# Five drains of GpSimd's DMA queue: four among the expert blocks, one behind the tail's gather

## The chip, the core and the metric

The kernel runs on one core of a Trainium2 chip. A core has a matrix engine (PE, with its weight loads as PEld), a vector engine (DVE), a scalar engine (ACT), GpSimd (POOL), a queue that mostly issues transfers (SP), and 16 DMA engines that all of these feed. The metric is the device time of one execution in microseconds (us), lower is better. A change is told from no change here when the median moves by more than about 0.5%, which is 5.9 us.

## The reference

The program computes one residual block of a streaming encoder for 512 tokens of width 1024 in float32: a layer norm, a token mixer (a gated MLP branch and a gated delta-rule branch, merged through gates), a second layer norm, a mixture of experts, and a last layer norm. Only the mixture of experts and the norm behind it matter here:

```
pg  = softmax(x @ w_rg + b_rg)            # one of 4 groups per token
le  = (x @ w_re + b_re) of that group     # 8 experts, the best two are taken
gate = p_group * softmax(top two logits)
y   = silu(x @ w1[e]) * (x @ w3[e]) @ w2[e]   for the two experts e of each token
out = sum over the two of gate * y
h   = LayerNorm(alpha * h + out)
```

There are 32 experts with 1024 x 512, 1024 x 512 and 512 x 1024 weights in float32, so 6 MB of weights each.

## The kernel before

The first half of the program (to about 676 us) is the token mixer, the norm behind it and the router, which sorts the experts by load and makes the lists of token indices. Then `Experts.run` goes through 32 expert blocks. For each it loads six 1 MB pieces of weights on SP's queue, gathers the block's token rows from `h1_dram` (`fetch`, L1605, an indirect DMA that POOL issues into one of the tiles called `mh`), turns them around on PE (`turn_x`, L1631), multiplies (`up`, L1659), applies the gate (`gate`, L1668), multiplies again (`down`, L1690), copies the result into the tile `once` (L1717 on DVE, L1722 on ACT) and scatters its rows to `y_rows` in DRAM (`store_y`, `scatter`, L1697, indirect DMAs that POOL issues). The order on each engine in this part is the order in which the code is written.

POOL's work here is nearly all DMA issues. In iteration b of the loop it meets, in this order: `fetch(b+3, 0)`, the gather of the first 64 rows of the block three ahead; for some blocks `fetch(b+2, 1)`, a further gather of up to 96 rows, which stands in a conditional and is skipped where the block has at most 64 tokens (L1602; the branch that skips it holds an instruction INC_SWDGE_SEM, which makes up the semaphore counts of the gather that was left out); and the scatters of block b-1. Blocks of even number from 4 to 26 are "short": they scatter 32 rows with one DMA (its index list is `itail`), the others up to block 27 use three DMAs (`itail` and twice `islot`), and the last four blocks none, since their results stay on the chip.

From block 25 on, `Tail` joins in. At (29, 1), that is at the end of iteration 29, it starts to add the experts' rows up: ACT's queue reads `y_rows` back in four pieces, and POOL gathers one more set of rows of it into `mh` (L1764, the helper's line is L1794). Behind that gather on POOL stand only small power operations for the last layer norm (L1838) and, at the very end, the scatter of the last 128 rows to `out` (L1788).

After the tail, each engine reads a flag and branches (L2028, L2029) past a part for token counts that the fixed plan doesn't hold; that part isn't entered with these inputs. On POOL the branch not entered also has an INC_SWDGE_SEM. Then comes the end of the program (L2120), where every engine has DRAIN instructions and a barrier.

Of the kernel before, what the change touches and what calls it, by code (L numbers as in the profile page):

```python
# [41 lines left out]
FEW = range(4, 28, 2)  # L42
TURNS = ((3, 4, 21, 1, 7), (5, 4, 20, -1, 6), (4, 2, 14, -1, 4), (12, 2, 3, 1, 8))
OOB = 1e4


C_BU, C_BQ, C_BK, C_BV, C_BZ, C_BGA, C_BGB = (8 * i for i in range(7))
# [1112 lines left out]
class Router:  # L1160
# [234 lines left out]
    def rows(self, W, idx2, n, slot, tail):  # L1395
# [10 lines left out]
        for q in range(2):  # L1406
            v.tensor_scalar(y[64 * q:64 * q + 64], x[0:64], 2.0, q + OOB, op0=OP.mult, op1=OP.add)
        v.scalar_tensor_tensor(out=slot, in0=m, scalar=-OOB, in1=y, op0=OP.mult, op1=OP.add)
        t = W.tile([32, 3, w], F32, name="rt%d" % w)
# [43 lines left out]
class Experts:  # L1453
# [30 lines left out]
    def clear(self):  # L1484

        for t in [self.u[:, p] for p in range(NP)] + [self.y0[:, 0:256]] + self.y:
            n = t.shape[1] // 128
            self.nc.scalar.activation(out=t.rearrange("p (a n) -> p a n", a=n), in_=bc(self.cst["ident"], n, 1),
                                      func=AF.Copy, scale=0.0)

    def run(self, blocks, more=None, clear=None, tail=None):

        nc, kk, nb = self.nc, self.kk, len(blocks)
        steps = []
        for b in range(nb + 1):
            steps += [(b, c) for c in range(4)] if b < nb else []
            steps += [(b - 1, 4), (b - 1, 5)] if b else []
        if clear:  # L1500
            steps[0:14] = steps[1:14] + steps[0:1]
        conds, self.raw, todo = {}, {}, iter(steps)

        def load(n, always=False):
            for _, (b, c) in zip(range(n), todo):
                blk = blocks[b]
                if blk[5] and not always and b not in conds:
                    m = nc.values_load(blk[4][0], engines=(ET.SP,), min_val=0, max_val=NB,
                                       skip_runtime_bounds_check_because="counts of tokens")
                    conds[b] = m > 0  # L1510
                self.raw[b, c] = kk.load_big(blk[1]()[c], conds.get(b), self.once if clear and b + c == 0 else None)
                self.last, self.prior = kk.loaded, self.last

        more = more or iter(())
        self.blocks, self.s = blocks, [{} for _ in blocks]
        self.short = lambda b: bool(tail) and (b >= E - NL or b in FEW)
        if clear:
            load(15, True)
            load(1, True)
            kk.behind(self.last, [kk.normed])  # L1520
            load(2, True)
        else:
            load(len(kk.raws), True)
        if clear:
            for x in self.x:
                nc.gpsimd.memset(x[:, :, NA:96], 0.0)
            self.s[0]["r"], self.s[1]["r"] = [None], [None]
        for b in range(2 if clear else 0, min(3, nb)):
            self.fetch(b, 0)
        if clear:  # L1530
            clear()
        next(more, None)
        self.fetch(0, 1)

        self.turn_x(0, (lambda: self.up(0, None)) if clear else None)
        if not clear:
            next(more, None)
        if nb > 1:
            self.fetch(1, 1)
        for b in range(nb + 1):  # L1540
            if b + 3 < nb:
                self.fetch(b + 3, 0)
            if tail and b >= RT:
                tail(b, 0)
            if b < nb:
                self.parts(b, self.up)
                if tail and b in (RT, RT + 3):
                    n = kk.nraw % len(kk.raws)
                    kk.raws = kk.raws[n:] + kk.raws[:n]
                    self.spare, kk.raws, kk.nraw = kk.raws[0:2], kk.raws[2:], 0  # L1550
                    load(2)
                else:
                    load(3 if clear and b == 0 else 4)
                if clear and b == 0:
                    self.turn_x(1)
                elif clear and b == 1:
                    self.turn(0)
                self.gate(b)
            if clear and b == 0:
                next(more, None)  # L1560
            elif b + 1 < nb:
                self.turn_x(b + 1)
            if b + 2 < nb and not self.short(b + 2):
                self.fetch(b + 2, 1)
            next(more, None)
            if b:
                self.parts(b - 1, self.down)
                load(2)
            next(more, None)
            if b < nb and not (clear and b == 0):  # L1570
                self.turn(b)
            if b and not (tail and b == nb):
                self.store_y(b - 1, tail)
            next(more, None)
            if tail and b >= RT:
                tail(b, 1)
# [153 lines left out]
class Tail:  # L1730
# [8 lines left out]
    def __call__(self, b, at):  # L1739
        nc, kk, ex, r = self.nc, self.kk, self.ex, self.r  # L1740
        v, g, act, m = nc.vector, nc.gpsimd, nc.scalar, 128 - 32
        if (b, at) == (RT, 1):
            (self.g, self.b), (self.F, ex.Y) = ([x[:, i * D:(i + 1) * D] for i in range(2)] for x in ex.spare[0:2])
            act.dma_start(out=ex.Y[0:4], in_=kk.a["rows"][R_L1G:R_L2B + 1, :])
            v.memset(self.F, 0.0)
            self.gather(r.lgate, r.gd_dram, r.lidx2, 2 * T)
            self.gather(self.F, self.h1_dram, r.lidx, T)
        elif (b, at) == (RT + 1, 1):
            self.spread(0, ALPHA)
        elif b == RT + 2:  # L1750
            self.affine(self.f[2 * at:2 * at + 2])
        elif (b, at) == (RT + 3, 0):
            self.affine([self.F])
        elif (b, at) == (RT + 3, 1):
            self.spread(2, 1.0)
        elif (b, at) == (RT + 4, 0):
            self.y = ex.spare
            kk.behind(self.load(0), ex.stores)
            self.load(1)
        elif (b, at) == (RT + 4, 1):  # L1760
            self.add(0, 1)
            self.load(2)
            self.load(3)
            self.gather(self.O, self.y_dram, r.lother, 2 * T)  # L1764
        elif (b, at) == (RT + 5, 0):
            self.apply((0, 1), self.stats(0, 1))
        elif (b, at) == (RT + 5, 1):
            self.add(2, 3)
            v.scalar_tensor_tensor(out=self.F, in0=self.O, scalar=r.lgate[:, 1:2], in1=self.F, op0=OP.mult, op1=OP.add)
        elif (b, at) == (RT + 6, 0):  # L1770
            self.m = self.stats(2, 3)
        elif (b, at) == (RT + 6, 1):
            self.apply((2, 3), self.m)
            for t in range(NT):
                kk.stores.append(nc.sync.dma_start(out=kk.a["out"][t * 128:(t + 1) * 128, :], in_=self.f[t]))
                if t == 0:
                    kk.behind(kk.stores[0], [ex.prior])
            v.scalar_tensor_tensor(out=self.F[0:m], in0=ex.Y[0:m], scalar=r.lgate[0:m, 0:1], in1=self.F[0:m],
                                   op0=OP.mult, op1=OP.add)
        elif (b, at) == (E, 2):  # L1780
            F = self.F
            for q in range(4):
                f = F[m:128, q * 256:(q + 1) * 256]
                v.scalar_tensor_tensor(out=f, in0=ex.end[q * 32:(q + 1) * 32, 0:256], scalar=r.lgate[m:128, 0:1], in1=f,  # L1784
                                       op0=OP.mult, op1=OP.add)
            (rs, mean), = self.stats(F)
            self.norm(F, rs, mean)
            x = g.indirect_dma_start(out=kk.a["out"], out_offset=bass.IndirectOffsetOnAxis(ap=r.lidx, axis=0), in_=F,  # L1788
                                     in_offset=None, bounds_check=T - 1, oob_is_err=False)
            kk.behind(x, kk.stores)  # L1790
            kk.stores.append(x)
# [332 lines left out]
```

## Time and profile before

| | us |
|---|---|
| three timed runs | 1184.94, 1183.8, 1179.16 |
| their median | 1183.8 |
| the profiled execution's own time | 1181.13 |
| its span, first to last instruction | 1179.3 |
| PE busy in the span | 1048.8 (89%) |
| POOL busy in the span | 210.4 (18%) |
| DMA engines' share of the time, 870 to 1031 us | 1.02, at 402 GB/s |

The span is what the rows of the trace cover, and 1.8 us of the execution's time lie outside it. A row of a group gives a line of the code, the engine, the operation, the tiles written and read, the count, and the durations. Engine names with a q (POOLq, SPq) are the instructions of that engine's queue which aren't counted as busy: semaphore waits, branches, drains, DMA issues of SP and ACT. Rows of one line's instructions give minimum, median and maximum duration in ns and then the first and last start in us. Rows in order of time begin with start and duration in us; in brackets stands the time for which the engine sat idle before it, and what ended it. A DMA that POOL issues shows on POOL with the time of its issue alone; when its data has landed is seen from those who wait for it.

### The profile page before, as it was taken

The numbers are of one execution on the slowest core, as the hardware profiler recorded it, in microseconds if no ns is written. First come the engines' busy times: TensorE is split into PE (matmuls) and PEld (weight loads), VectorE is DVE, ScalarE is ACT, GpSimd is POOL, SyncE is SP. The second block draws the span as 40 slices with busy tenths as digits, with TensorE's granted clock in tenths as the row PEclk, the third lists the DMA queues.
The fourth block names the chain that finished last, engine by engine and source line by source line (L and its number), as shares of the span: only waits on it lengthen the run. The fifth ranks groups of instructions, "written<-read, shape, count | busy, mean of one in ns | idle before, by whom it ended". The sixth has DMA issues, their size and how long they took to land. (4 is left out here: it accounts for less than half of the span.)

```text
span 1179.3 us, 18779 instructions
## 1 busy us (share of the span) xinstructions
PE 1048.8 (89%) x7042; PEld 694.1 (59%) x7042; DVE 622.6 (53%) x1373; ACT 367.1 (31%) x805; POOL 210.4 (18%) x277
## 2 busy tenths in 40 slices
PE   5999999999999999999999977887998877979861
PEld 4888788867777777768887733433444333433320
DVE  8484444477667767773685653532232222233473
ACT  6243355444545455443532221101111010011100
POOL 3010100131321323120100113221132121021110
PEclk9999999999999999999999989887999896988855
DMA  6412423711212112112735789999999999999893
GB/s 227 151 63 81 161 89 100 237 40 57 70 54 70 56 55 71 38 55 104 294 151 225 294 315 406 384 401 400 373 379 402 401 404 399 402 395 414 334 419 130
DMA packets 55833, 268.30 MB, mean 228 GB/s; under 512 B 10859, under 2 KB 15243, under 8 KB 31656
## 3 DMA queue, kind: packets, MB, share of 16 engines
q1 hardware_dynamic: 44400, 246.96, 54.7%
q0 software_dynamic: 8144, 10.63, 2.9%
q10 hardware_dynamic: 3176, 9.20, 2.0%
q8 instruction: 72, 1.18, 0.4%
q14 instruction: 41, 0.34, 0.1%
HBM read 273.70 MB, written 21.00 MB: 250 GB/s over the span
## 5 line engine op out<-in xcount | busy, mean ns | idle before, releaser
L271 PE MATMUL psi<-hTh,hi 128*128 128x512 f32 x448 | 184.0, 413 | 0.0
L271 PE MATMUL psi<-hTh,lo 128*128 128x512 f32 x448 | 180.3, 403 | 0.3 <-DVE lo L271 0.3
L271 PE MATMUL psi<-hTl,hi 128*128 128x512 f32 x448 | 180.2, 403 | 0.0
L1669 DVE TENSOR_TENSOR h<-h,u 128x640 f32<-128x640 f32 (+1 forms) x32 | 17.7, 555 | 257.2 <-ACT h L1668 257.2
L271 DVE TENSOR_TENSOR lo<-raw,hi 128x1024 fp32r<-128x1024 f32 x74 | 92.5, 1250 | 75.2 <-ACT hi L271 75.0
L1659 PE MATMUL u<-raw,xs 128*32 128x256 f32 x1296 | 92.5, 419 | 27.7 <-DMA raw<-in_w 25.1
L271 ACT CAST hi<-raw 128x1024 fp32r<-128x1024 f32 x74 | 77.4, 1046 | 107.3 <-PE psi L271 89.9
L271 PEld LDWEIGHTS psi<-hTl,hi 128*128 128x128 f32 x448 | 84.5, 189 | 20.6 <-issue 3.0
L271 PEld LDWEIGHTS psi<-hTh,hi 128*128 128x128 f32 x448 | 84.4, 189 | 20.3 <-issue 3.3
L271 PEld LDWEIGHTS psi<-hTh,lo 128*128 128x128 f32 x448 | 84.6, 189 | 18.5 <-issue 1.8
L1668 ACT ACTIVATE h<-u 128x640 f32<-128x640 f32 (+1 forms) x32 | 15.7, 491 | 230.1 <-PE u L1659 113.5
L1659 PEld LDWEIGHTS u<-raw,xs 128*32 128x32 f32 x1296 | 43.2, 117 | 69.6 <-DMA raw<-in_w 34.4
L1659 PE MATMUL u<-raw,x 128*64 128x512 f32 x304 | 70.8, 611 | 8.4 <-DVE rt L1414 6.0
L1697 POOL DMA_INDIRECT y_rows<-once,itail x28 | 26.1, 931 | 280.8 <-DVE once L1717 235.4
L1678 ACT COPY hT<-t 128x128 f32<-128x128 f32 x32 | 8.5, 267 | 174.8 <-PE t L1675 161.4
L1717 DVE COPY once<-yz 32x256 f32<-32x256 f32 x112 | 46.7, 417 | 19.6 <-PE yz L1690 16.5
L271 DVE SCALAR_TENSOR_TENSOR acc<-xp,cols,acc 128x512 f32<-128x512 f32 x72 | 54.0, 750 | 5.4 <-ACT acc L271 4.3
L1659 PEld LDWEIGHTS u<-raw,x 128*64 128x64 f32 x304 | 25.8, 142 | 49.1 <-issue 43.1
L1690 PE MATMUL yz<-raw,hT 128*32 128x256 f32 x560 | 46.0, 473 | 9.0 <-DMA raw<-in_w 7.1
L1690 PE MATMUL y<-raw,hT 128*64 128x512 f32 x160 | 40.2, 647 | 4.9 <-DMA raw<-in_w 1.9
L271 POOL TENSOR_TENSOR rk<-ssk,mhalf 128x4 f32<-128x4 f32 x8 | 10.0, 1251 | 177.9 <-DVE ssk L271 177.9
L1605 POOL DMA_INDIRECT mh<-h_dram,idx x36 | 35.3, 980 | 17.3 <-issue 9.7
(517 smaller groups left out, 1958.0 us busy)
## 6 DMA issues: line engine op xcount, KB each, us to landing
raw<-in_w SPq DMA_DIRECT2D x144, 1024.0 KB
raw<-in_wt SPq DMA_DIRECT2D x73, 512.0 KB
rawl<-in_w SPq DMA_DIRECT2D x24, 1024.0 KB
rawh<-in_w SPq DMA_DIRECT2D x23, 1024.0 KB
raw<-in_wv SPq DMA_DIRECT2D x8, 512.0 KB
y_rows<-zero SPq DMA_DIRECT2D x8, 512.0 KB
raw<-y_rows ACTq DMA_DIRECT2D x4, 1024.0 KB
rawl<-in_wo SPq DMA_DIRECT2D x3, 1024.0 KB
```

Of the source, the lines that this page charges most:

```text
L271: op._ins = getattr(getattr(self.nc, op.attr), op.name)(*map(real, op.args), **{k: real(x) for k, x in op.kw.items()})
L1605: self.nc.gpsimd.indirect_dma_start(out=x, out_offset=None, in_=self.h1_dram, in_offset=bass.IndirectOffsetOnAxis(ap=self.blocks[b][2 + i] ...
L1659: self.nc.tensor.matmul(self.u[q * r:(q + 1) * r, NP if p is None else p, 0:c], x[:, k, r0:r0 + r], self.raw[b, k // 2][:, o:o + c], start ...
L1668: self.nc.scalar.activation(out=h, in_=u[:, :, 0], func=AF.Silu)
L1669: self.nc.vector.tensor_mul(out=h, in0=h, in1=u[:, :, 1])
L1678: self.nc.scalar.copy(out=x[:, n], in_=self.t[1][:, 0:128])
L1690: self.nc.tensor.matmul(y[q * r:(q + 1) * r, 0:c], t[:, i, j * r:(j + 1) * r], self.raw[b, 4 + k // 2][:, o:o + c], start=k == 0, stop=k == 3)
L1697: x = self.nc.gpsimd.indirect_dma_start(out=out, out_offset=bass.IndirectOffsetOnAxis(ap=idx, axis=0), in_=src, in_offset=None, bounds_che ...
L1717: nc.vector.tensor_copy(out=small[:, q], in_=src)
```

## The change

A `drain` is an instruction on POOL's queue that moves no data. Four are put into `Experts.run`, at the head of iterations 6, 12, 18 and 24 (only in the main run over the 32 blocks, which is the one with `clear`). Since the iteration before ends with `store_y` and this one begins with `fetch`, each stands behind the `itail` scatter of a short block (4, 10, 16, 22) and ahead of the gather for block 9, 15, 21 or 27. A fifth stands in `Tail`, behind the gather of `y_rows` rows at (29, 1) and ahead of the power operations of the tail's norms. Apart from these five, each engine has the same instructions in the same order as before.

```
--- before.py
+++ after.py
@@ -42,6 +42,7 @@
 OOB = 1e4
+DRAINS = 6, 12, 18, 24
@@ -1538,6 +1539,8 @@
         if nb > 1:
             self.fetch(1, 1)
         for b in range(nb + 1):
+            if clear and b in DRAINS:
+                nc.gpsimd.drain()
             if b + 3 < nb:
                 self.fetch(b + 3, 0)
@@ -1762,6 +1765,7 @@
             self.load(2)
             self.load(3)
             self.gather(self.O, self.y_dram, r.lother, 2 * T)
+            g.drain()
         elif (b, at) == (RT + 5, 0):
```

More of the change, by code (lines that the diff above doesn't have):

```diff
@@ L44 @@
 OOB = 1e4
+DRAINS = 6, 12, 18, 24
 C_BU, C_BQ, C_BK, C_BV, C_BZ, C_BGA, C_BGB = (8 * i for i in range(7))
@@ L1540, in run @@
         for b in range(nb + 1):
+            if clear and b in DRAINS:
+                nc.gpsimd.drain()
             if b + 3 < nb:
@@ L1764, in __call__ @@
             self.gather(self.O, self.y_dram, r.lother, 2 * T)
+            g.drain()
         elif (b, at) == (RT + 5, 0):
```

## The prediction

> **What bounds the kernel now.** The change touches POOL's queue alone, so I read from the end of the span backwards, to see whether POOL ends anything. The last rows of the chain of waits (start, duration, what):
>
> ```profile
> 1161.99 1.30 DVE raw L1844
> ...
> 1163.63 0.99 POOL out L1788
> ```
>
> The chain of busy work stops at 1164.6 us, but the span is 1179.3 us: for 14.7 us no engine computes. The busy times by stage confirm it (the last two figures of a row are the DMA engines' share and GB/s):
>
> ```profile
> 1164.00:1170.00 6.00, 0.00 (x0) 0.00 (x0) 0.00 (x0) 0.00 (x0) 0.62 (x1) 0.50 0.08 30
> 1170.00:1179.30 9.30, 0.00 (x0) 0.00 (x0) 0.00 (x0) 0.00 (x0) 0.00 (x0) 0.50 0.00 0
> ```
>
> From 1170 us on nothing moves either. What fills this stretch are queue instructions, so I asked for those of L2029 (the branch behind the tail) and of L2120 (the program's end):
>
> ```profile
> L2029 POOLq EVENT_SEMAPHORE  x6: 17/30/43, 1164.2 to 1166.9; - x6
> ...
> L2029 POOLq INC_SWDGE_SEM  x1: 2370/2370/2370, 1167.0 to 1167.0; - x1
> ...
> L2120 SPq EVENT_SEMAPHORE  x14: 17/28/28, 1169.3 to 1179.2; - x14
> ...
> L2120 POOLq DRAIN  x3: 46/102/9060, 1169.4 to 1179.0; - x3
> L2120 SPq DRAIN  x3: 7/7/13, 1170.0 to 1178.7; - x3
> ```
>
> POOL's last semaphore wait, behind which the scatter to `out` has landed, ends at 1166.9 us. Then POOL's INC_SWDGE_SEM takes 2.37 us, and its first DRAIN 9.06 us (1169.4 to 1178.4); the other engines' drains take some ns, and all wait in the barrier for POOL. These two instructions, 11.43 us, are on the path that sets the end, and nothing covers them. The same DRAIN at the program's start, with no DMA issued yet, is short, and so is INC_SWDGE_SEM:
>
> ```profile
> L2116 POOLq INC_SWDGE_SEM  x1: 31/31/31, 0.1 to 0.1; - x1
> ...
> L2116 POOLq DRAIN  x1: 174/174/174, 0.3 to 0.3; - x1
> ```
>
> What is different at the end? No transfer is pending; but POOL has issued 110 DMAs since. INC_SWDGE_SEM tells how the queue's past enters. It stands ten times in the branch that skips a gather, and its durations there, taken stage by stage (one row of an answer for each), are:
>
> ```profile
> L1602 POOLq INC_SWDGE_SEM  x1: 380/380/380, 682.6 to 682.6; - x1
> ...
> L1602 POOLq INC_SWDGE_SEM  x1: 860/860/860, 771.4 to 771.4; - x1
> ...
> L1602 POOLq INC_SWDGE_SEM  x1: 1380/1380/1380, 882.2 to 882.2; - x1
> ...
> L1602 POOLq INC_SWDGE_SEM  x1: 1900/1900/1900, 998.9 to 998.9; - x1
> ```
>
> The number of DMAs that POOL issues comes from the list of DMA issues:
>
> ```profile
> DA<-g_dram POOLq DMA_DIRECT2D x8, 256.0 KB
> ...
> mh<-h_dram,idx POOLq DMA_INDIRECT x36
> ...
> y_rows<-once,islot POOLq DMA_INDIRECT x32
> y_rows<-once,itail POOLq DMA_INDIRECT x28
> ...
> g_dram<-gr POOLq DMA_DIRECT2D x1, 16.0 KB
> ...
> gd_dram<-gt POOLq DMA_DIRECT2D x1, 8.0 KB
> lgate<-gd_dram,lidx POOLq DMA_INDIRECT x1
> raw<-h_dram,lidx POOLq DMA_INDIRECT x1
> mh<-y_rows,lother POOLq DMA_INDIRECT x1
> out<-raw,lidx POOLq DMA_INDIRECT x1
> ```
>
> 36 + 32 + 28 + 8 + 6 = 110. In POOL's order of time 10 had been started at the first of the ten (g_dram, eight DA, one gather), 34 at 771.4, 60 at 882.2, 86 at 998.9 and 110 at 1167.0. 380, 860, 1380, 1900 and 2370 ns lie on a line: (2370 - 380) / 100 = 20 ns per DMA ever issued, and some 170 ns at none. I read this as a walk over a list that grows with each DMA and that nothing shortens, although these DMAs had landed long before. If the first DRAIN at the end walks the same list, it costs (9060 - 46) / 110 = 82 ns per entry; the 46 ns is the shortest drain, which comes after it, with nothing issued between.
>
> **The change part by part.** It removes nothing, adds five drains, and moves nothing else.
>
> *The end.* If a drain empties the list, then behind the fifth only the scatter to `out` is new, one entry. INC_SWDGE_SEM falls from 2370 to about 170 + 20 = 190 ns (bounds: 31 ns by the row with nothing issued, 380 by the row with ten): -2.2 us (-2.0 to -2.3). The DRAIN falls from 9060 to about 46 + 82 = 130 ns (bounds: 46 and 174 by the short rows): -8.9 us (-8.9 to -9.0). Together -11.1 us, between -10.9 and -11.4 if the list is what is paid for.
>
> *The drains among the blocks.* No row shows a drain with a transfer under way. I take it that it waits for the landing of the scatter ahead of it, and walks the list. 31 DMAs have been issued ahead of the first, then 19, 20 and 19 between them: 31 x 82 ns = 2.5 us, and 1.6 us for each of the others. The scatter's landing is seen where DVE waited for it, and in the chain:
>
> ```profile
> 854.81 1.71 DVE L1717 COPY once<-yz 32x256 f32<-32x256 f32 x4 [1.57 <-DMA y_rows<-once,itail]
> ...
> 1103.32 7.17 DMA y_rows<-once,islot
> ```
>
> The `itail` scatter issued at 846.99 had landed by 854.81, 7.8 us after its start; an `islot` one took 7.2. So a drain ends 7.8 us after the start of its scatter if the walk runs beside the wait, or at worst 7.8 + 2.5 = 10.3 us (first) and 9.4 us (others) if it comes behind. Below, the first place, the second and the fourth (the third lies between them), each with scatter, gather behind it, and POOL's next instruction:
>
> ```profile
> 757.46 0.91 POOL L1697 DMA_INDIRECT y_rows<-once,itail  x1 [7.52 <-DVE once L1717]
> 758.67 0.95 POOL L1605 DMA_INDIRECT mh<-h_dram,idx  x1 [0.30 <-issue]
> 769.30 0.89 POOL L1697 DMA_INDIRECT y_rows<-once,itail  x1 [9.68 <-DVE once L1717]
> ...
> 846.99 0.89 POOL L1697 DMA_INDIRECT y_rows<-once,itail  x1 [12.94 <-DVE once L1717]
> 848.19 0.96 POOL L1605 DMA_INDIRECT mh<-h_dram,idx  x1 [0.30 <-issue]
> 856.80 0.88 POOL L1697 DMA_INDIRECT y_rows<-once,itail  x1 [7.65 <-DVE once L1717]
> ...
> 1022.65 0.89 POOL L1697 DMA_INDIRECT y_rows<-once,itail  x1 [21.08 <-DVE once L1717]
> 1023.85 0.96 POOL L1605 DMA_INDIRECT mh<-h_dram,idx  x1 [0.31 <-issue]
> 1031.17 0.88 POOL L1697 DMA_INDIRECT y_rows<-once,itail  x1 [6.36 <-DVE once L1717]
> ```
>
> Two things are queued behind a drain. The next scatter: at the first place the drain ends at 765.3 to 767.8, the gather's issue 1.3 later, 0.2 us or more ahead of 769.30. At the second it ends at 854.8 to 856.4, the gather's issue at 856.1 to 857.7, against 856.80: 0 to 0.9 us late. At the fourth 1030.5 to 1032.1, then 1031.8 to 1033.4 against 1031.17: 0.6 to 2.2 us late. A late scatter holds only the tile `once`, whose next copies come a block later. The other thing is the gather: it slips by about 6 to 9 us. It is used three blocks on; the tightest is the first, gathered at 758.67 for block 9, whose transposes on PE are
>
> ```profile
> 782.68 0.71 PE L1631 MATMUL t<-ident,mh 64*128 64x64 f32 x8
> ```
>
> 24.0 us later. Issued at 767.8 at the latest, and landing within some 8 to 10 us (my estimate from the scatters' 7 to 8), it is there about 5 us early. I take nothing for the four, with 0 to 3 us (0.9 + 2.2) as the cost if the late scatters passed straight to the end. A gain there I exclude: INC_SWDGE_SEM gets shorter in the middle too, but POOL waits for DVE after each.
>
> *The fifth drain.* Its neighbours, and a read of the same rows on ACT's queue in the chain:
>
> ```profile
> 1111.13 7.93 DMA raw<-y_rows
> ...
> 1111.46 1.05 POOL L1794 DMA_INDIRECT mh<-y_rows,lother  x1 [7.13 <-PE u L1659]
> 1124.46 1.68 POOL L1838 TENSOR_TENSOR tr<-tv,mhalf 128x1 f32<-128x1 f32 x1 [11.95 <-DVE tv L1835]
> ```
>
> It waits for a gather started at 1111.46; if that lands in about 8 us as its neighbour did, and 20 entries are walked (1.6 us), it ends at 1119.4 to 1121.1, at least 3.3 us ahead of the power operation, which waits for DVE until 1124.46. Cost 0; each us beyond those 3.3 would delay DVE's norm.
>
> Sum: the profiled execution, 1181.1 us, falls by 11.1 to 1170.0. The median of the runs stands 2.7 us above that execution, so I forecast 1183.8 - 11.1 = 1172.7 us, 0.94% less.
>
> **The rivals.**
>
> *The end's drain has a fixed price* (8%). Only one drain in the trace comes after DMAs, so 9.06 us could be what any drain pays once something has been issued. For it: 174, 102 and 46 ns are all drains on an untouched or just drained queue. Against it: the straight growth of INC_SWDGE_SEM on the same queue. Then only the 2.2 us go: 1181.6 us, no change that can be told.
> [...]
>
> *A drain waits but leaves the list* (4%). Then nothing is saved: 1183.8 plus 0 to 3, at most 1186.8. Against it: the two POOL drains behind the long one, 102 and 46 ns, found nothing left to walk.
>
> *Slower: the fixed price, paid five times on POOL's queue* (4%). If every drain took 7.8 us for the landing and 9.06 us behind it, plus 1.3 for the gather, the next scatter would start 18.2 us after the one ahead, where the rows leave 11.8 (769.30 - 757.46), 9.8 and 8.5 us: late by 6.4, 8.4 and 9.7, the third place like the second, and the power operation by 3.9 (1111.46 + 16.9 against 1124.46): 37 us. Passed on in full, less 2.2, this gives 1218.6 us. How much of it the buffers of the next blocks would hide, no row says; slower by over 5.9 us needs 8 of the 37 to get through.
>
> **How the numbers follow.** The forecast has 84%. Its own spread is that of the runs before (1179.16 to 1184.94, moved by 11.1: 1168.1 to 1173.8), widened at the top by the 3 us: 1167.5 to 1177. The range takes in part of the fixed-price case, to 1179.5, and leaves out its upper half and the two cases above. Faster by over 0.5%: 0.83; within 0.5%: 0.13, the two cases without a saving and a little of the forecast's edge; slower: 0.04.
>
> **What would show it.** Right: in the rows of L2120 no POOL drain over 0.3 us; INC_SWDGE_SEM at L2029 near 0.2 us; the span's end about 1.3 us behind the landing of `out` (1179.3 - 1166.9 = 12.4 before); INC_SWDGE_SEM at L1602 no longer growing past 0.8 us; and the new drains 6 to 10 us long, with the scatter behind them within 2 us of its old distance. Wrong: an end drain still near 9 us (fixed price, or the list kept), or POOL's power operation at L1838 starting behind its input, or PE waiting for `mh` at L1631. A drain's length that follows the number of DMAs since the last would carry the whole reasoning.

## The result, and the profile after

The changed kernel takes 1169.65 us, the median of five runs (1167.66 to 1171.56). The kernel before, run beside it, takes 1179.71 us (1179.16 to 1184.94, the three runs of the prediction and two more). The ratio is 0.990, with a 95% interval of 0.987 to 0.993. The medians differ by 10.1 us; 11.1 were forecast.

The profiled execution of the changed kernel takes 1169.69 us with a span of 1167.8 us, against 1181.13 and 1179.3. What lies outside the span is as before (1.9 and 1.8 us). Where did the 11.4 us between the two executions go? First the end, in the form of the prediction's rows: lines have moved by some, so that L2029 is now L2033 and L2120 is L2124.

```profile
L2033 POOLq EVENT_SEMAPHORE  x6: 17/30/43, 1163.3 to 1166.0; - x6
...
L2033 POOLq INC_SWDGE_SEM  x1: 192/192/192, 1166.0 to 1166.0; - x1
...
L2124 SPq EVENT_SEMAPHORE  x14: 17/28/28, 1166.2 to 1167.8; - x14
L2124 POOLq EVENT_SEMAPHORE  x4: 17/17/17, 1167.0 to 1167.7; - x4
L2124 POOLq DRAIN  x3: 52/102/135, 1166.3 to 1167.5; - x3
L2124 SPq DRAIN  x3: 7/7/13, 1166.9 to 1167.2; - x3
```

INC_SWDGE_SEM fell from 2370 to 192 ns and POOL's longest DRAIN from 9060 to 135 ns: 11.10 us less, as the sum had it. The end behind the landing of `out` did not shorten by all of that. It fell from 12.4 us (1166.9 to 1179.3) to 1.8 us (1166.0 to 1167.8), by about 10.5 (10.6 by these rounded times; the 11.44 us between the executions, less the 0.92 us explained below, give 10.52). The missing 0.6 us stand in the rows of SP and POOL. POOL's drain ends at 1166.4, but POOL's first barrier semaphore comes only at 1167.0, right behind SP's drain of 1166.9, to which SP's own list of semaphore instructions leads. That list starts when POOL's INC_SWDGE_SEM ends (1169.3 before, 1166.2 now), beside POOL's DRAIN, and reaches SP's drain 0.7 us later. In the kernel before it ran in the shade of POOL's drain: SP's drain stood at 1170.0, and POOL's first semaphore followed POOL's drain at once, at 1178.5:

```profile
L2120 POOLq EVENT_SEMAPHORE  x4: 17/17/17, 1178.5 to 1179.2; - x4
```

The rest of the difference, 0.92 us, lies ahead of the end: the scatter to `out` is issued earlier (1163.57 before, 1162.65 now). Executions of one kernel differ by more than that (1167.66 to 1171.56), so I don't count it as an effect.

The five drains (rows of their two lines), and INC_SWDGE_SEM in the branch that skips a gather, at three of the stages quoted before, where it took 860, 1380 and 1900 ns:

```profile
L1543 POOLq DRAIN  x4: 6792/7239/7545, 757.0 to 1021.3; - x4
L1768 POOLq DRAIN  x1: 8971/8971/8971, 1107.5 to 1107.5; - x1
...
L1605 POOLq INC_SWDGE_SEM  x1: 245/245/245, 770.8 to 770.8; - x1
...
L1605 POOLq INC_SWDGE_SEM  x1: 385/385/385, 881.1 to 881.1; - x1
...
L1605 POOLq INC_SWDGE_SEM  x1: 505/505/505, 997.7 to 997.7; - x1
```

By the prediction's line, 170 + 20 ns per DMA, these three rows stand for 4, 11 and 17 DMAs. By POOL's order of time it had issued 3, 10 and 16 since the drain ahead, and 34, 60 and 86 in all. So the count that shows in these lengths starts afresh at each of the drains.

Now POOL's instructions at the first, second and fourth place, in order of time, and PE's first transposes for block 9:

```profile
757.29 0.90 POOL L1700 DMA_INDIRECT y_rows<-once,itail  x1 [7.59 <-DVE once L1720]
765.77 0.96 POOL L1608 DMA_INDIRECT mh<-h_dram,idx  x1 [7.58 <-issue]
768.49 0.89 POOL L1700 DMA_INDIRECT y_rows<-once,itail  x1 [1.76 <-DVE once L1720]
...
846.14 0.89 POOL L1700 DMA_INDIRECT y_rows<-once,itail  x1 [12.89 <-DVE once L1720]
853.59 0.95 POOL L1608 DMA_INDIRECT mh<-h_dram,idx  x1 [6.56 <-issue]
854.85 0.88 POOL L1700 DMA_INDIRECT y_rows<-once,itail  x1 [0.30 <-issue]
...
1021.51 0.89 POOL L1700 DMA_INDIRECT y_rows<-once,itail  x1 [21.27 <-DVE once L1720]
1029.37 0.96 POOL L1608 DMA_INDIRECT mh<-h_dram,idx  x1 [6.97 <-issue]
1030.64 0.88 POOL L1700 DMA_INDIRECT y_rows<-once,itail  x1 [0.30 <-issue]
...
781.87 0.71 PE L1634 MATMUL t<-ident,mh 64*128 64x64 f32 x8
```

The gather, which used to follow its scatter by 0.3 us, now waits 6.6 to 7.6 us ("issue": for nothing that the profile names, which here is the drain). At the first place the next scatter still waits for DVE, 1.76 us: there is room left. At the second and the fourth it follows the gather at once, so POOL's queue holds it up. The distance from scatter to scatter is 8.7 us at the second (9.8 before) and 9.1 at the fourth (8.5 before, so 0.6 late). The gather for block 9, issued at 765.77, is used at 781.87, 16.1 us later, and PE's row shows no wait. Nowhere in the changed kernel does PE wait for a gather into `mh`.

The stream of weights goes on through the stretch that holds the third and the fourth drain as it did (the same window before: 1.02, 402):

```profile
870.00:1031.00 161.00, 134.98 (x1270) 61.25 (x1264) 47.82 (x101) 15.65 (x36) 31.95 (x34) 0.90 1.02 404
```

Behind the tail's gather the drain ends at 1107.5 + 8.97 = 1116.5, and the power operation starts 6.4 us later, when DVE has its input ready:

```profile
1107.75 1.05 POOL L1798 DMA_INDIRECT mh<-y_rows,lother  x1 [7.32 <-PE u L1662]
1122.93 1.67 POOL L1842 TENSOR_TENSOR tr<-tv,mhalf 128x1 f32<-128x1 f32 x2 [14.13 <-DVE tv L1839]
```

### The profile page after: what moved, and what is told of

It is laid out like the page before. It is cut to its first block, busy times and chain, and to the rows that moved or that the text cites. A ratio compares the mean times of both kernels' runs of the same rounds, so it can differ in the third digit from the quotient of the medians.

```text
span 1167.8 us, 18784 instructions
## 1 busy us (share of the span) xinstructions
PE 1042.6 (89%) x7042; PEld 692.6 (59%) x7042; DVE 623.3 (53%) x1373; ACT 366.7 (31%) x805; POOL 209.7 (18%) x277
## 2 busy tenths in 40 slices
DMA packets 55833, 268.30 MB, mean 230 GB/s; under 512 B 10859, under 2 KB 15243, under 8 KB 31656
## 3 DMA queue, kind: packets, MB, share of 16 engines
q0 software_dynamic: 8144, 10.63, 2.9%
## 5 line engine op out<-in xcount | busy, mean ns | idle before, releaser
L1662 PE MATMUL u<-raw,xs 128*32 128x256 f32 x1296 | 89.9, 410 | 31.3 <-DMA raw<-in_w 26.7
L1662 PEld LDWEIGHTS u<-raw,xs 128*32 128x32 f32 x1296 | 42.8, 115 | 70.7 <-DMA raw<-in_w 34.2
L1662 PE MATMUL u<-raw,x 128*64 128x512 f32 x304 | 70.8, 611 | 9.3 <-DVE rt L1414 5.6
L1662 PEld LDWEIGHTS u<-raw,x 128*64 128x64 f32 x304 | 25.4, 142 | 50.3 <-issue 41.6
```

The source lines that it names most:

```text
L1662: self.nc.tensor.matmul(self.u[q * r:(q + 1) * r, NP if p is None else p, 0:c], x[:, k, r0:r0 + r], self.raw[b, k // 2][:, o:o + c], start ...
```

## The experiments

My theory: the queue keeps an entry for each DMA that POOL has issued; INC_SWDGE_SEM and DRAIN walk the entries at 20 and 82 ns each (worked out from the 380 to 2370 ns and the 9060 ns of the kernel before), a DRAIN removes them, and its price is nothing where POOL would be idle. No row shows a list or a walk; they are my picture of these lengths. Below, entries are the DMAs that such a length counts, n in 170 + 20 n or 46 + 82 n ns, and a walk is the second of these times. The rivals: the price is fixed and paid by the first drain; the price follows bytes or the time since the last drain; the drains act in another way, by what they do to the blocks. All comparisons are of medians, with the kernel before run on the same chip; ratios come with 95% intervals.

### The drain behind the tail's gather alone

```
-DRAINS = 6, 12, 18, 24
+DRAINS = ()
```

> Only the drain behind the tail's gather stays; the four among the blocks are taken out. Theory of the list (an entry per DMA, walked by a drain and emptied by it): the drain now finds 109 entries instead of 20. In the changed kernel it ended 0.86 us behind the gather's landing, 41 ns an entry; by that it ends 4.5 us behind it, some 12.5 us after its start, at about 1120 us, and at the full 82 ns per entry 8.9 us behind, at about 1124.6, just about where the power operation starts. Either way the end is as short as with five drains (INC_SWDGE_SEM 0.19 us, DRAIN 0.13 us) and the time is that of the changed kernel, about 1169.7 us, at most 1 us more. Rival (the four are needed, since a long walk in the tail holds the power operation and with it the vector engine): the power operation starts behind its input and the time lies 2 us or more above the changed kernel's.

Measured: 1169.43 us against 1180.52, ratio 0.9906 (0.9884 to 0.9928). One drain does what five do. It now has 109 DMAs ahead of it. Its row among those of its line, and below it POOL's instructions around it in order of time:

```profile
L1768 POOLq DRAIN  x1: 12586/12586/12586, 1109.1 to 1109.1; - x1
```

```profile
1109.35 1.05 POOL L1798 DMA_INDIRECT mh<-y_rows,lother  x1 [7.30 <-PE u L1662]
1123.82 1.67 POOL L1842 TENSOR_TENSOR tr<-tv,mhalf 128x1 f32<-128x1 f32 x2 [13.43 <-DVE tv L1839]
```

It ends at 1121.7, 2.1 us ahead of the power operation, which still waits for DVE. So the four drains among the blocks are not needed for the saving; they only make the fifth 3.6 us shorter, where nothing waits for it.

### The four alone

```
             self.gather(self.O, self.y_dram, r.lother, 2 * T)
-            g.drain()
```

> The four drains among the blocks stay, the fifth is taken out. Theory of the list: 21 entries are left at the end (110 less 89), so INC_SWDGE_SEM takes 170 + 21 x 20 = 590 ns and the end's DRAIN 46 + 21 x 82 = 1770 ns, 2.0 us more than with five drains: about 1171.7 us. Rival (fixed price of the end's drain once enough has been issued): DRAIN near 9 us, time near 1178.

Measured: 1170.71 us against 1180.52, ratio 0.9918 (0.9897 to 0.9939). 21 DMAs have been issued since the last drain:

```profile
L2032 POOLq INC_SWDGE_SEM  x1: 590/590/590, 1165.7 to 1165.7; - x1
...
L2123 POOLq DRAIN  x3: 52/102/1768, 1166.3 to 1168.7; - x3
```

The rows are those of the branch behind the tail and of the program's end, as in all runs below. 170 + 21 x 20 = 590 and 46 + 21 x 82 = 1768: the line through none and 110 holds in between. A fixed price cannot give this.

### The first alone

```
-DRAINS = 6, 12, 18, 24
+DRAINS = (6,)
...
-            g.drain()
```

> Only the first of the five drains (head of iteration 6) stays. Theory of the list: 79 entries are left at the end (110 less 31): INC_SWDGE_SEM 170 + 79 x 20 = 1750 ns, DRAIN 46 + 79 x 82 = 6520 ns; 3.2 us less than the kernel before, so about 1176.5 us. Rival (the price follows how long ago the last drain was, or the bytes moved, most of which by GpSimd's queue come after it alike): no straight line through 1, 21, 79 and 110 entries.

Measured: 1177.46 us against 1180.52, ratio 0.9972 (0.9961 to 0.9984), 3.1 us less. 79 DMAs follow the drain:

```profile
L2032 POOLq INC_SWDGE_SEM  x1: 1750/1750/1750, 1167.8 to 1167.8; - x1
...
L2123 POOLq DRAIN  x3: 52/102/6510, 1169.6 to 1176.6; - x3
```

The 31 DMAs ahead of a drain at the 757th microsecond are worth 3.1 us at the end of the program, over 400 us later. That a drain has happened does not matter; how many DMAs follow it does (79 here, 110 before: 6510 and 9060 ns).

### A drain with nothing under way

To the kernel before, one drain, moved from behind the tail's gather to behind DVE's statistics, when the gather has long landed:

```
         elif (b, at) == (RT + 5, 0):
-            self.apply((0, 1), self.stats(0, 1))
+            m = self.stats(0, 1)
+            g.drain()
+            self.apply((0, 1), m)
```

> The kernel before with one drain, later in the tail: behind the two power operations of iteration 30, when the gather ahead has landed about 7 us ago. Theory of the list: nothing is left to wait for, so the drain takes the bare walk of 109 entries, 46 + 109 x 82 = 8980 ns; it ends at about 1136, before the next power operation at 1141, so it is covered, and the time is the changed kernel's, about 1169.7 us. If the 41 ns per entry seen behind a landing were the price of the walk, the drain would take 4.5 us; if it takes 9.0, then half of the walk ran beside the wait in the changed kernel. Rival (what a drain costs is the wait for the landing alone): below 0.3 us.

Measured: 1167.85 us against 1180.52, ratio 0.9909 (0.9885 to 0.9933).

The drain's row, and POOL's instructions in order of time:

```profile
L1767 POOLq DRAIN  x1: 11133/11133/11133, 1121.9 to 1121.9; - x1
```

```profile
1121.82 2.22 POOL L1840 TENSOR_TENSOR tr<-tv,mhalf 128x1 f32<-128x1 f32 x2 [14.15 <-DVE tv L1837]
1137.82 1.07 POOL L1840 TENSOR_TENSOR tr<-tv,mhalf 128x1 f32<-128x1 f32 x2 [13.78 <-DVE tv L1837]
```

The drain's row starts while the power operations ahead still run, until 1124.04. It ends at 1133.03, 9.0 us behind them; 46 + 109 x 82 ns = 8.98 us. That is the walk with no transfer left to wait for: the gather was started at 1106.62, and in the changed kernel, by the semaphore events of its trace, the same gather landed 7.9 us after its start, so at about 1114.5 here (my estimate). The next power operations start 4.8 us after its end, when DVE lets them. The work of the program's end has been moved whole to a place where POOL idles.

### The same drain without cover

To the kernel before, one drain on the end path itself, between the last statistics and the scatter to `out`:

```
             (rs, mean), = self.stats(F)
+            g.drain()
             self.norm(F, rs, mean)
```

> The kernel before with one drain in the worst place: behind the last power operation, ahead of the scatter to the output, where the last 128 rows wait for it. Theory (it is the cover that saves, not the drain): the drain takes 46 + 109 x 82 = 8980 ns, starting beside the vector engine's last operation of 1.3 us, so it delays the scatter by about 7.5 us, and the end saves 11.1: about 3.5 us less than the kernel before, near 1176 us. Rival (a drain costs nothing in itself and helps wherever it stands): the time of the changed kernel, about 1169.7.

Measured: 1177.99 us against 1179.6, ratio 0.9981 (0.9971 to 0.9991), 1.6 us less; I had expected 3.5.

The same two views:

```profile
L1787 POOLq DRAIN  x1: 10485/10485/10485, 1158.9 to 1158.9; - x1
```

```profile
1158.94 1.46 POOL L1839 TENSOR_TENSOR tr<-tv,mhalf 128x1 f32<-128x1 f32 x1 [16.48 <-DVE tv L1836]
1170.42 1.05 POOL L1789 DMA_INDIRECT out<-raw,lidx  x1 [10.03 <-issue]
```

The drain's row starts with the power operation ahead of it and ends at 1158.9 + 10.49 = 1169.39, again 9.0 us behind that operation's end (1160.40). The scatter, which followed the power operation by 1.61 us of idle time in the changed kernel, follows by 10.03: 8.4 us late, where I had expected 7.5. With the 10.5 us that the end gives, this makes 2.1 us, inside the interval (1.1 to 3.4). So it is the cover that saves: the same drain in line with the end path pays most of the price that it removes.

### A drain at the head of every block

```
-DRAINS = 6, 12, 18, 24
+DRAINS = tuple(range(3, 29))
```

> Drains at the head of every iteration from 3 to 28, 26 instead of four, with the fifth. Each holds GpSimd's queue until the scatters ahead have landed, 6 to 8 us. Theory (the gathers three blocks ahead and the scatters have room): the end is as short, the weights' stream goes on at about 400 GB/s, and the time lies within 2 us of the changed kernel's. Rival (held queue): behind the blocks with three scatters the gather and the conditional gather come 6 to 8 us late each time, the next scatter too, and the matrix engine waits for its transposes: 3 to 20 us more than the changed kernel.

Measured: 1167.08 us against 1179.6, ratio 0.9891 (0.9872 to 0.9909).

```profile
L1543 POOLq DRAIN  x26: 6073/9194/12725, 718.1 to 1089.2; - x26
```

A drain's row begins ahead of the end of the issue before it (in the changed kernel at 757.0, with an issue from 757.29 to 758.19). From the end of the last issue to the end of the drain POOL's queue stands still for 5 to 9.5 us each time, 181 us in all, about half of the stretch, and the time does not get longer. But that is not because the gathers have room, as the theory had it. The first half of the rival came true: PE waited for the further gathers of five blocks (L1645), up to 9.9 us each:

```profile
PE t L1645 <- DMA mh<-h_dram,idx: 34.0, 5, 9.9
```

What did not come true is the price. The stream of weights moved as much in the same 400 us, in the changed kernel (first row) and here:

```profile
690.00:1090.00 400.00, 336.67 (x3024) 154.78 (x3022) 135.74 (x309) 47.82 (x106) 90.11 (x93) 0.91 1.01 395
690.00:1090.00 400.00, 323.45 (x2986) 153.95 (x2986) 132.32 (x306) 47.79 (x105) 87.43 (x91) 0.90 1.01 395
```

With the DMA engines full in both, PE would else have waited for weights in part of that time: its waits for the weights' tile `raw` at L1662 are 17.5 us here and 27.8 us in the changed kernel. So this run shows that the time bears 26 drains, not that nothing waits for them.

### Twenty small DMAs

To the kernel before, no drain, but 20 more DMAs of 8 KB from POOL's queue, DRAM to DRAM, which nothing uses:

```
             if b + 3 < nb:
                 self.fetch(b + 3, 0)
+            if clear and 4 <= b < 24:
+                nc.gpsimd.dma_start(out=kk.small[b - 4], in_=kk.g_dram[0:16, :])
```

> The kernel before with 20 more DMAs on GpSimd's queue, 8 KB each from DRAM to DRAM, one in each iteration from 4 to 23; nobody reads what they write. Theory (the price is per DMA, whatever it moves): 130 entries at the end: INC_SWDGE_SEM 170 + 130 x 20 = 2770 ns, DRAIN 46 + 130 x 82 = 10710 ns; 2.0 us more at the end. Their issues, about 1 us each, lie in GpSimd's idle time, so about 2 us more in all than the kernel before. Rival (the price follows bytes or descriptors): these DMAs are small beside the gathers and scatters, 0.16 MB of 10.6, so 2370 and 9060 ns stay within 2%.

Measured: 1170.4 us against 1179.6, ratio 0.9924 (0.9901 to 0.9947). More DMAs made the kernel faster, which neither theory had said.

```profile
L1604 POOLq INC_SWDGE_SEM  x1: 2300/2300/2300, 997.7 to 997.7; - x1
...
L2032 POOLq INC_SWDGE_SEM  x1: 367/367/367, 1166.5 to 1166.5; - x1
...
L2123 POOLq DRAIN  x3: 46/102/812, 1166.9 to 1168.3; - x3
```

At 997.7 us all DMAs still count: 86 + 20 entries give 2290 ns. At the end 130 DMAs have been issued, but 367 ns stand for 10 entries and 812 ns for 9. Between those two places some 120 DMAs ceased to count, without a drain.

### Eight and eleven small DMAs

The same with `4 <= b < 12` and with `4 <= b < 15`, 118 and 121 DMAs in all, to find where the 120 cease to count. I then believed that it happened at the 121st DMA.

> The kernel before with 8 of the 20 small DMAs, 118 in all. With twenty, the 121st DMA's issue took 1.90 us instead of 1.03 and the end found only 10 entries; so the list holds 120 and empties itself when it is full, for less than 1 us. By that theory 118 never fill it: INC_SWDGE_SEM 170 + 118 x 20 = 2530 ns, DRAIN 46 + 118 x 82 = 9720 ns, so 0.8 us more at the end than before, about 0.1% slower, not told apart in time. Rival (price by bytes): 2370 and 9060 ns. Rival (the small DMAs as such put the list in another state, without any limit): an end below 1 us.

> The kernel before with 11 of the small DMAs, 121 in all: the 121st is the very last one, the scatter to the output. If the limit is 120 entries by count, its issue takes some 0.9 us more (1.9 instead of 1.05), and the end finds 1 entry: INC_SWDGE_SEM 0.19, DRAIN 0.13 us, about 10 us less than the kernel before in all. Rival (the limit counts descriptors or bytes, of which the small DMAs have few): the list isn't full yet, INC_SWDGE_SEM 170 + 121 x 20 = 2590 and DRAIN 46 + 121 x 82 = 9970 ns, about 1 us slower than before.

Measured: 1181.8 us (ratio 0.9999, 0.9983 to 1.0015) and 1182.43 us (1.0017, 1.0002 to 1.0031), both against 1180.58.

```profile
L2032 POOLq INC_SWDGE_SEM  x1: 2530/2530/2530, 1169.7 to 1169.7; - x1
...
L2123 POOLq DRAIN  x3: 46/102/9713, 1172.3 to 1182.5; - x3
```

```profile
L2032 POOLq INC_SWDGE_SEM  x1: 2590/2590/2590, 1165.8 to 1165.8; - x1
...
L2123 POOLq DRAIN  x3: 46/102/9956, 1168.4 to 1178.9; - x3
```

The first set is with 118, the second with 121. Eight DMAs of 8 KB lengthen the two instructions by 160 and 653 ns, 20 and 82 ns each, as much as the kernel's own 110 DMAs, which move 10.63 MB, 97 KB on average: the price is per DMA, not per byte. And at 121 all of them still counted: my place was wrong.

### The changed kernel, and the drain at every block, side by side

The two unchanged, on one chip.

> The changed kernel again, for a comparison on one chip with the next one: 10 us below the kernel before.

> The kernel with a drain in every iteration from 3 to 28 again, beside the changed kernel on one chip. Theory (drains under cover are free, and nothing is left to gain at the end, where the changed kernel's two instructions take 0.33 us): the same time as the changed kernel within 1 us. Rival (the earlier draining also helps in the blocks): 2 us or more below it.

Measured against 1180.58: 1169.2 us (0.9906, 0.9879 to 0.9932) and 1167.1 us (0.9883, 0.9858 to 0.9908). The second is 2.1 us lower, as it had been in separate runs, but the intervals overlap and so do the single runs (1166.71 to 1175.21, 1165.46 to 1172.13). Whether 26 drains are better than five stays open. In that kernel the median of INC_SWDGE_SEM in the blocks is 176 ns, near the 170 that the line has at no DMA (382 ns in the changed kernel, 710 before):

```profile
L1605 POOLq INC_SWDGE_SEM  x10: 167/176/401, 683.2 to 1013.2; - x10
```

### Forty small DMAs

Two per iteration, 150 DMAs in all, to tell whether the DMAs cease to count by number or for another reason. In the profile's count of packets the 40 add 32 packets each, 16 of them under 512 bytes (57113 and 11499 against 55833 and 10859 before).

```
             if b + 3 < nb:
                 self.fetch(b + 3, 0)
+            if clear and 4 <= b < 24:
+                for i in range(2):
+                    nc.gpsimd.dma_start(out=kk.small[2 * b - 8 + i], in_=kk.g_dram[0:16, :])
```

> The kernel before with 40 of the small DMAs, two in each iteration from 4 to 23, 150 DMAs in all. With 20 of them the list lost about 120 of its 130 entries between the 106th DMA and the end; with 11 it held all 121. So it empties itself somewhere from the 122nd DMA on. Theory (by count): it happens from the 122nd to the 130th DMA, which is now in block 21 or 22, and about 120 entries go, so about 30 are left at the end: INC_SWDGE_SEM 770 ns, DRAIN 2.5 us, 8 us less than the kernel before. Rival (by room: the small DMAs, with one piece of 512 bytes for each of 16 DMA engines, need less of it than the gathers and scatters): it happens near the same place in the program as with 20, so about 10 to 15 are left at the end: INC_SWDGE_SEM below 0.5 us, DRAIN below 1.3 us, 9 us or more less.

Measured: 1173.87 us against 1181.58, ratio 0.9934 (0.9917 to 0.9951), 7.7 us less.

```profile
L1605 POOLq INC_SWDGE_SEM  x1: 2705/2705/2705, 998.0 to 998.0; - x1
...
L2033 POOLq INC_SWDGE_SEM  x1: 762/762/762, 1165.4 to 1165.4; - x1
...
L2124 POOLq DRAIN  x3: 102/193/2445, 1166.2 to 1169.5; - x3
```

2705 ns stand for some 126 entries, so all DMAs still counted then. 762 and 2445 ns stand for 30 and 29: of 150, again 120 went. With the 9 or 10 that were left of 130 this looks like a matter of number: some 120 went in both, after the 126th DMA or so (all counted here) and by the 130th (the last with twenty), if it is the same place in both. The issue of 1.90 us that I had taken for the place is none: here the 141st DMA, at the same place in the program (1063.85 us), takes 1.92 us. What makes them go, whether all at once, and at which DMA exactly, no run shows.

## Why the prediction held, point by point

*The list, and its two prices.* The prices per DMA are shown, and that a drain sets the count back. That there is a list which is walked is my picture of it; no row shows the list itself. The DMAs counted are POOL's own; the other issues in the traces of the kernel before and of the changed one are SP's and ACT's, and PE and DVE have none. The prediction had the prices from one drain and a row of INC_SWDGE_SEM; the kernels above give six lengths of the list at the program's end:

| entries | INC_SWDGE_SEM, ns | 170 + 20 n | longest DRAIN, ns | 46 + 82 n |
|---|---|---|---|---|
| 1 (changed kernel) | 192 | 190 | 135 | 128 |
| 21 (the four alone) | 590 | 590 | 1768 | 1768 |
| 79 (the first alone) | 1750 | 1750 | 6510 | 6524 |
| 110 (before) | 2370 | 2370 | 9060 | 9066 |
| 118 (eight small) | 2530 | 2530 | 9713 | 9722 |
| 121 (eleven small) | 2590 | 2590 | 9956 | 9968 |

"A list that nothing shortens" was wrong: with 130 and with 150 DMAs some 120 no longer counted at the end. This kernel issues 110, and there all of them counted (2370 and 9060 ns), so its forecast did not depend on it. With 20 more the end's two instructions took 1.2 us (367 and 812 ns), so the drains would have had no more than that to save.

*The end, -11.1 us.* The two instructions gave 11.10. What failed is the step from there to the span: I left out that SP's semaphore list, which starts at the end of INC_SWDGE_SEM and takes 0.7 us, would be last once POOL's DRAIN was shorter than it. It takes 0.6 us back, so that the span ends 1.8 us behind the landing of `out` where I had said 1.3. The true term is -10.5.

*The drains among the blocks, 0 (0 to 3).* The cost is not to be seen: with the four, without them, and with 26 the medians are 1169.65, 1169.43 and 1167.08 us. Whether the walk runs beside the wait for the landing or behind it was left open. By my working it does some of both. The drains ended 7.3, 6.6 and 7.0 us behind the start of their scatters at the first, second and fourth place, below the 7.8 us that I had taken for the landing alone, because the scatters landed sooner: from the semaphore events of the trace I work out 5.7 to 6.2 us, and that the drains with 19 to 31 entries ended 0.8 to 1.3 us behind the landing, about 41 ns per entry, half of the 82. The drain with 109 entries fits: it ended 12.4 us behind its gather's start, by the events of its own trace that gather landed in 7.9 us, and 4.5 us are left, 41 ns for each entry. This is worked out, not shown by a row.

*What is queued behind them.* The scatter at the fourth place was 0.6 us late, the low end of the 0.6 to 2.2 forecast; the second was not late by its distance (0 to 0.9 forecast). The gather for block 9 was in place: no wait on PE. With 26 drains gathers were late, and PE waited 34 us for them; the stream of weights, with the DMA engines full (1.01), hid that.

*The fifth drain, 0.* It ended 8.8 us behind the gather's start (7.9 to 9.6 forecast), with 6.4 us to spare before the power operation.

*The base.* Four later sets of runs put the kernel before at 1179.6 to 1181.6 us, and the first one, with two runs more, at 1179.71: the 1183.8 of three runs lay some 3 us high. So the forecast of 1172.7 was 3 us above the 1169.65 measured, although the difference was 1 us too large. Against the profiled execution, the working had given 1170.0, and 1169.69 was measured. That this is so close is luck in part: the end gave 10.5 us and not 11.1, and the 0.9 us by which the scatter to `out` came earlier, which nothing in the working forecast, made up for it.

*The rivals.* A fixed price is refuted by the 1768 and 6510 ns drains. A drain that keeps the list is refuted by the 135 ns. The slower case needed five prices of 9 us behind the landing; the drains among the blocks cost 0.8 to 1.3 there, and even 26 of them did not lengthen the time. But a drain that the end waits for does cost its price: the run without cover gave up 8.4 of 10.5 us to it.

## What to carry to other kernels

Look at the first DRAIN and the INC_SWDGE_SEM of POOL's queue at the program's end: here they took 9060 and 2370 ns, and their lengths told how many DMAs GpSimd had issued since the last drain (82 and 20 ns each, up to some 126 DMAs), as much for DMAs of 8 KB as for the others, and also for the 31 issued over 400 us before the end. One drain of GpSimd's queue, placed behind its last DMA but one, where the next POOL instruction stood idle for 13.4 us until DVE let it start, took 11.1 us off the time; placed in line with the end it took off 1.6 us. Ahead of gathers that others need, look whether they come late and what hides it: here it was the stream of weights. When a long last instruction goes, look for what ran in its shade on the other queues: what ends last there is the new end, and the saving is less by that much.

## What the runs showed of the hardware that I had not expected

Kernels with 110, 118 and 121 DMAs of GpSimd and no drain paid for all of them at the end (9060, 9713, 9956 ns), those with 130 and 150 only for 9 or 10 and 29 or 30 (812 and 2445 ns). So in these two some 120 ceased to count, later than the 126th or so, which still counted (2705 ns), and by the 130th if it is the same place in both. That is why 20 DMAs that do nothing saved nearly as much (9.2 us, 1170.4 against 1179.6) as a drain (11.1 us, 1169.43 against 1180.52), which is a matter of this count and not a method.

The row of a drain on POOL's queue also began while the operation ahead still ran: at 1121.9, with that operation's end at 1124.04, and without cover at 1158.9, with the end at 1160.40. So the rows say 11.13 and 10.49 us, but from that end to the drain's own it is 9.0 us in both places, what 109 DMAs give by 46 + 82 n (8.98).
